# Starting every SBUF buffer of a hybrid FoX and mLSTM block at a multiple of 64 bytes, and loading its gate columns through two queues

## The chip, the core and the metric

The kernel runs on one core of one Trainium2 chip. The metric is the device time of one execution in microseconds (us), lower is better. A time is given as the median of several executions; the profile is one further execution, recorded by the hardware profiler.

## What is computed

One layer of a decoder block over 16 meta tokens and 512 real ones. Cut to what matters here:

```python
h = rms_norm(x, g_pre)                     # 528 x 1024
z = h @ w_in                               # 1024 x 14352, then split:
(fq, fk, fv, ff, fz, mqk, mv, mi, mf, mo, mz, ga, gb) = jnp.split(z, SPLIT_POINTS, axis=-1)
oa = forgetting_attention(fq, fk, fv, log_sigmoid(ff + b_fox_f))       # 8 heads of 128
ya = (oa * silu(fz)) @ w_a
mq, mk = jnp.split(silu(causal_conv(mqk, conv_w, conv_b)), 2, axis=-1)
hb = mlstm_scan(mq * 256 ** -0.5, mk, mv, mi + b_i, log_sigmoid(mf + b_f))   # 4 heads, values of 512
hb = rms_norm(sigmoid(mo) * hb, g_head)
yb = (hb * silu(mz)) @ w_b
return x + rms_norm((sigmoid(ga) * ya + sigmoid(gb) * yb) @ w_o, g_post)
```

The gates `ff`, `mi` and `mf` are 8, 4 and 4 columns of the input projection, 16 in all.

## The kernel before

**Precision.** Nearly every product is made of three matmuls (`mm3`, L128 to L131): each fp32 operand is split in a high part (a copy by ScalarE, names ending in `h`) and a low part (the rest, a subtraction by VectorE, names ending in `l`), and high x high, high x low and low x high are summed in PSUM. `wsplit` (L116) does this for a block of weights that `wload` (L102) fetched as `raw` tiles of 512 KB on SyncE's DMA queue. So a weight block is fetched, copied by ScalarE, subtracted by VectorE, and read by TensorE.

**Stages.** The start fetches the gain `g`, the token blocks `x` (into `yb`), the first value weights `wv_r` and the gate columns `wg_raw`; normalises block after block (`stat_part`, `scale_part`, `norm_part`: sum of squares on ScalarE, `rs` on GpSimd by a power, scaling on VectorE, transposes `tr` on TensorE, then `hh` and `hl`); and multiplies each block with the first 256 value columns and the 16 gate columns together (`pv`, 272 columns). The four mLSTM heads follow (convolved `pqk`, scores `ps`, values `pna`/`pnb`, gates `po` and `pz`, output `pyb`), then the FoX heads and the output projection `pout`.

**The meta tokens** have their own small operand `hm`, written by three engines (L513 to L515), and a projection `pvm` (`proj_m`, L168). `gn` collects the gate columns of the four real blocks and of the meta block; eight transposes (L542, L543) turn those of the real blocks into the rows `pgf` and `pgi`, two more (L545) those of the meta block into `pgm`, and one (L547) the convolution's taps into `gct`, copied to `gc`. From the rows VectorE and ScalarE work out the log gates (L555 to L566: `fx`, `gi`, exponential, logarithm), running sums (L571) and running maxima (L585), all of 12 partitions in `yb`. In the same stretch VectorE forms `l`, `t1l` and `t2l` (`st_tokens`, L181: sums of blocks of the tokens that later products use), and the low halves of the weights.

**Order.** A scheduler places the instructions of each engine after a cost model, except those wrapped in `pin`, which keep their program order. DMAs are issued in program order on the queue of the engine that starts them: SyncE for most, ScalarE for `g` and `wg_raw`.

**Buffers.** Tiles are laid out one behind another in SBUF. A statistics tile is one float per partition (4 bytes), a row of values is 514 floats. In the built kernel those lengths put the begin of the tiles behind them at other residues: `hh`, `hl`, `hm`, `big_h`, `big_l`, `qk1h`, `qk1l`, `vh` and the tail of `yb` views are at 32 beyond a multiple of 64 bytes, the weight tiles, `vl`, `y` and the `t1` to `t4` tiles at a multiple of 64. No DMA of this kernel is started by GpSimd.

Of the kernel before, what the change touches and what calls it, by code (L numbers as in the profile page):

```python
# [8 lines left out]
F32 = mybir.dt.float32  # L9
# [39 lines left out]
def tile_hybrid_block(ctx: ExitStack, tc: tile.TileContext, x, meta, norm_pre, norm_post, w_in, b_fox_f,  # L49
# [30 lines left out]
    gc = cp.tile([P, 96], F32, name="gc")  # L80
    col = cp.tile([P, NB + 2 * NCH, 12], F32, name="col")

# [235 lines left out]
    wg_raw = sb([P, KC, 16], F32, "t3l", "wg_raw", mw)  # L318
    for i in (1, 0):
        rows = slice(i * 512, i * 512 + 512)  # L320
        for o, c in ((0, C_FF), (8, C_MI)):
            nc.scalar.dma_start(wg_raw[:, 4 * i:4 * i + 4, o:o + 8], win[rows, c:c + 8].rearrange("(k p) n -> p k n", p=P))
# [15 lines left out]
    def stat_part(b):  # L338
        xt, n = xs[b]
        junk = sb([P, 2, 512], BF16, "vh", f"junk{b}")  # L340
        ss = sb([P, 1], F32, "ss", f"ss{b}", bufs=5)
        if b == 0:
            half = sb([P, 1], F32, "rs", "ss_half", bufs=5)
# [8 lines left out]
        rs = sb([P, 1], F32, "rs", f"rs{b}", bufs=5)  # L352
        pin(G.tensor_tensor(rs[:n], ss[:n], mhalf[:n], ALU.pow))
        rstd.append(rs)
# [34 lines left out]
    def v_tiles(h):  # L389
        vh = sb([P, NCH, MV + 2], F32R, "vh", f"vh{h}")  # L390
        vl = sb([P, NCH, MV + 2], F32R, "vl", f"vl{h}")
        vm = sb([P, MV + 2], F32R, "vm", f"vm{h}")
# [104 lines left out]

    b_fr = cp.tile([12, 1], F32, name="b_fr")
    b_ir = cp.tile([12, 1], F32, name="b_ir")
    V.memset(b_ir, 0.0)  # L500
# [27 lines left out]
    for b in range(NCH):  # L528
        pg = pv0[b]
        for d, o, n in ((0, 256, 8), (8, 268, 4), (20, 264, 4)):  # L530
            V.tensor_copy(gn[:, b, d:d + n], pg[:, o:o + n])
        S.activation(vh[:, b, 0:256], pg[:, 0:256], AF.Copy)
        V.tensor_tensor(vl[:, b, 0:256], pg[:, 0:256], f(vh[:, b, 0:256]), ALU.subtract)
    pm = psum1("pvm00")
    proj_m(pm[:, 0:NG], w0, NG)
# [3 lines left out]
    w_first.append(wsplit(lk, pin))  # L539
    pf, pi, pm2 = psum1("pgf"), psum1("pgi"), psum1("pgm")  # L540
# [39 lines left out]
    mp = cp.tile([12, NCH], F32, name="mp")  # L580
    V.tensor_tensor_scan(mx[:, 0:NM], a[:, 0:NM], a[:, 0:NM], 0.0, ALU.max, ALU.max)
# [128 lines left out]
    def mo_part(h):  # L710
        so = sb([P, NCH, MV], F32, "w", f"so{h}")
        pn = banks(f"po{h}", NCH)

        snaps = [so.rearrange("p s (m n) -> p m s n", m=2)[:, m] for m in range(2)]
        units = [(pn[m], pn[2 + m], snaps[m], slice(m * P, m * P + P)) for m in range(2)]
        st_products(st_wide(C_MO + h * MV, f"wo{h}"), units)

        dry = sb([P, 1], F32, "ss", f"dry{h}", bufs=5)
# [19 lines left out]
    def value_part(h, wpk, v, so, hts, chunks):  # L738
        wh, wl = wpk
        vh, vl, vm = v  # L740
        for c in chunks:
            pn = (psum1(f"pna{h}{c}"), psum1(f"pnb{h}{c}"))
            for u in (1, 0):
                o, n = u * 256, 256 + 2 * u
                for j in range(c + 1):
# [5 lines left out]
                         start=False, stop=True)  # L751
            r = sb([P, 1], F32, "r", f"r{h}{c}", bufs=4)
            V.tensor_scalar(r, pn[1][:, 256:257], -1.0, col[:, NB + NCH + c, 8 + h:9 + h], ALU.mult, ALU.max)
# [8 lines left out]
            junk = sb([P, MV], BF16, "y", f"mjunk{h}{c}", bufs=2)  # L762
            ss = sb([P, 1], F32, "ss", f"mss{h}{c}", bufs=5)
            S.activation(junk, ht, AF.Square, accum_out=ss)
            V.tensor_scalar(ss, ss, 1.0 / MV, EPS, ALU.mult, ALU.add)
            rs = sb([P, 1], F32, "rs", f"mrs{h}{c}", bufs=5)
            G.tensor_tensor(rs, ss, mhalf, ALU.pow)
# [39 lines left out]
    for h in range(MH):  # L807
        if pend is not None:
            bt = turn_part(*pend)
        q = conv_part(h, 0)  # L810
        k = conv_part(h, 1)
        if h:
# [3 lines left out]
        if h == 0:  # L816
            v = v0
            w1 = v_chunk(0, 1)
            ps = banks("pv01", 2)
# [81 lines left out]
    def prob_part(p, m, q, k):  # L901
# [7 lines left out]
        for c in range(NCH):  # L909
# [4 lines left out]
            parts = [(0, kn)] if kn <= 512 else [(0, HL), (HL, kn)]  # L914
            mn = sb([P, 2], F32, "mn", f"mn{h}{c}", bufs=4)
            for i, (s0, s1) in enumerate(parts):
# [194 lines left out]
```

## Time and profile before

| | |
|---|---|
| median of 3 executions | 963.04 us (962.84 to 963.21) |
| the profiled execution | 963.74 us |
| its span in the trace | 962.0 us |
| TensorE busy | 944.3 us, 98% of the span, 5720 matmuls |
| VectorE busy | 572.3 us, 59% |
| ScalarE busy | 439.5 us, 46% |
| GpSimd busy | 140.1 us, 15% |
| bytes read from HBM | 86.95 MB, 93 GB/s over the span |

Engines are named PE (TensorE's matmuls), PEld (its weight loads), DVE (VectorE), ACT (ScalarE), POOL (GpSimd); SPq and ACTq are the queues of SyncE and ScalarE that start DMAs. In a timeline row the first number is the start and the second the duration, both in us; brackets at the end tell how long the engine had been idle and what released it. The duration of a matmul is its way through the array; the rate of a series is read from start to start.

### The profile page before, as it was taken

How to read it: one execution, taken by the hardware profiler on the slowest of the kernel's cores; microseconds unless marked ns; L12 is line 12 of the kernel's file. 1: busy time of each engine (PE TensorE's matmuls, PEld its weight loads, DVE VectorE, ACT ScalarE, POOL GpSimd, SP SyncE). 2: the span in 40 equal slices, each digit the busy share in tenths (PEclk: the TensorE clock that was granted, in tenths of full speed). 3: DMA queues.
4: the chain of work that ended last, by engine and by line, in shares of the span. 5: the costliest groups of instructions: out<-in, count | busy, mean ns of one | idle time of the engine just before them, and what ended most of it. 6: DMA issues, size and time to landing. Idle time of an engine off the chain costs nothing.

```text
span 962.0 us, 14294 instructions
## 1 busy us (share of the span) xinstructions
PE 944.3 (98%) x5720; PEld 837.4 (87%) x5720; DVE 572.3 (59%) x966; ACT 439.5 (46%) x740; POOL 140.1 (15%) x186
## 2 busy tenths in 40 slices
PE   8999899999999999999999999999999999999997
PEld 6998899889998899988999888898888888888887
DVE  6898588447786288862788445445345454444433
ACT  5646456436564255562555224456235365422331
POOL 3054100122001220011112010123111012100000
PEclk9999899999999999999999999999999999999999
DMA  7222143303323123322224242333332332523202
GB/s 224 91 70 77 45 132 100 88 22 96 118 73 105 60 66 111 110 59 84 81 79 166 87 137 66 106 89 111 88 96 94 88 87 68 175 88 103 95 22 89
DMA packets 71469, 90.05 MB, mean 94 GB/s; under 512 B 4965, under 2 KB 56261, under 8 KB 71402
## 3 DMA queue, kind: packets, MB, share of 16 engines
q1 hardware_dynamic: 69288, 89.06, 30.2%
q8 instruction: 45, 0.74, 0.3%
q10 hardware_dynamic: 2114, 0.07, 0.1%
q14 instruction: 22, 0.18, 0.1%
HBM read 86.95 MB, written 2.16 MB: 93 GB/s over the span
## 4 chain that ended last, share of the span: by engine, by line
PE 89%; DVE 4%; ACT 2%; issue 1%; POOL 1%; DMA 1%; ACTq 0%; POOLq 0%; DVEq 0%; SPq 0%
PE pyb L131 3%; PE pyb L129 3%; PE pyb L130 3%; PE pz L130 3%; PE pz L131 3%; PE pz L129 3%; PE pv L129 3%; PE pv L131 3%; PE pv L130 3%; PE pqk L129 2%; PE pqk L131 2%; PE pqk L130 2%; PE po L130 2%; PE po L129 2%; PE po L131 2%; PE pfk L131 2%
## 5 line engine op out<-in xcount | busy, mean ns | idle before, releaser
L928 POOL TENSOR_SCALAR pn<-lt,rsum 128x128 f32<-128x128 f32 x32 | 23.1, 723 | 213.2 <-DVE rsum L926 213.2
L129 PE MATMUL pyb<-bh,wb_h 128*128 128x512 f32 x128 | 50.8, 397 | 0.0
L131 PE MATMUL pyb<-bh,wb_l 128*128 128x512 f32 x128 | 50.7, 396 | 0.0
L130 PE MATMUL pyb<-bl,wb_h 128*128 128x512 f32 x128 | 50.7, 396 | 0.0
L130 PE MATMUL pv<-wv_l,hh 128*128 128x512 f32 (+1 forms) x128 | 47.2, 368 | 1.7 <-DVE wv_l L123 1.5
L129 PE MATMUL pv<-wv_h,hh 128*128 128x512 f32 (+1 forms) x128 | 46.9, 367 | 0.0
L131 PE MATMUL pv<-wv_h,hl 128*128 128x512 f32 (+1 forms) x128 | 46.7, 365 | 0.0
L660 DVE SCALAR_TENSOR_TENSOR y<-z,gc,y 128x512 f32<-128x512 f32 (+1 forms) x48 | 35.9, 752 | 2.2 <-ACT y L653 1.5
L129 PE MATMUL pqk<-hh,wk_h 128*128 128x264 f32 x128 | 36.4, 285 | 0.0
L129 PE MATMUL pfk<-hh,wfk_h 128*128 128x264 f32 x128 | 36.4, 284 | 0.0
L131 PE MATMUL pfk<-hh,wfk_l 128*128 128x264 f32 x128 | 36.4, 284 | 0.0
L129 PE MATMUL pqk<-hh,wq_h 128*128 128x258 f32 x128 | 36.4, 284 | 0.0
L131 PE MATMUL pqk<-hh,wk_l 128*128 128x264 f32 x128 | 36.3, 284 | 0.0
L130 PE MATMUL pqk<-hl,wk_h 128*128 128x264 f32 x128 | 36.3, 284 | 0.0
L130 PE MATMUL pfk<-hl,wfk_h 128*128 128x264 f32 x128 | 36.3, 283 | 0.0
L130 PE MATMUL pqk<-hl,wq_h 128*128 128x258 f32 x128 | 36.0, 282 | 0.0
L131 PE MATMUL pqk<-hh,wq_l 128*128 128x258 f32 x128 | 36.0, 282 | 0.0
L129 PE MATMUL pout<-wo_h,mh 128*128 128x256 f32 (+1 forms) x96 | 30.6, 319 | 0.0
L131 PE MATMUL pout<-wo_h,ml 128*128 128x256 f32 (+1 forms) x96 | 30.5, 318 | 0.0
L130 PE MATMUL pout<-wo_l,mh 128*128 128x256 f32 (+1 forms) x96 | 30.4, 317 | 0.0
L925 ACT ACTIVATE lt<-lt,mn 128x144 f32<-128x144 f32 (+3 forms) x32 | 18.4, 574 | 24.7 <-DVE mn L920 24.6
L130 PEld LDWEIGHTS pv<-wv_l,hh 128*128 128x128 f32 x128 | 24.1, 188 | 6.3 <-DVE wv_l L123 2.1
(979 smaller groups left out, 3299.8 us busy)
## 6 DMA issues: line engine op xcount, KB each, us to landing
wv_r<-in_w_in_dram SPq DMA_DIRECT2D x16, 512.0 KB, 4.5
wo_r<-in_w_in_dram SPq DMA_DIRECT2D x16, 512.0 KB, 4.5
wz_r<-in_w_in_dram SPq DMA_DIRECT2D x16, 512.0 KB, 3.8
wb_r<-in_w_b_dram SPq DMA_DIRECT2D x16, 512.0 KB, 3.5
ab<-d_na SPq DMA_DIRECT2D x8, 672.0 KB, 4.0
wq_r<-in_w_in_dram SPq DMA_DIRECT2D x8, 512.0 KB, 3.8
wk_r<-in_w_in_dram SPq DMA_DIRECT2D x8, 512.0 KB, 3.7
wfq_r<-in_w_in_dram SPq DMA_DIRECT2D x8, 512.0 KB, 3.9
```

The lines of the kernel that those rows point to most:

```text
L129: T.matmul(ps, ah, bh, start=start, stop=False, **kw)
L130: T.matmul(ps, ah, bl, start=False, stop=False, **kw)
L131: T.matmul(ps, al, bh, start=False, stop=stop, **kw)
L660: V.scalar_tensor_tensor(y[:, t0:L], z[:, m, t0 + j:L + j], gc[:, j * 16 + mi:j * 16 + mi + 1], y[:, t0:L], ALU.mult, ALU.add)
L925: S.activation(lt[:, 0:kn], lt[:, 0:kn], AF.Exp, bias=mn[:, li:li + 1], scale=-1.0, accum_out=rsum)
L928: G.tensor_scalar(pn[:, o:o + P].rearrange("p (g t) -> p g t", g=4), lt[:, 0:32].unsqueeze(1).to_broadcast([P, 4, 32]), rsum, None, ALU.mult)
```

## The change

- A helper `line` gives every small tile a length of 16 floats (64 bytes) or a multiple, and the rows of the value tiles `vh`, `vl`, `vm` get 16 more floats where they had 2. GpSimd's DMA scratch area is 1 KB instead of 16 KB. In the built kernel every buffer then begins at a multiple of 64 bytes.
- The four DMAs that fetch `wg_raw` are split: the two of the rows 512 to 1023 stay on ScalarE's queue, the two of the rows 0 to 511 are started by SyncE, behind `x` block 1.
- The six gate transposes of the first three blocks stand ahead of the meta projection `pvm`, those of the fourth behind it, as all eight did.
- The second block of value weights of head 0 (`v_chunk(0, 1)`) is split ahead of the key convolution instead of behind it.

```diff
+    def line(pool, name, n=1, parts=P, **kw):
+        return pool.tile([parts, -(-n // 16) * 16], F32, name=name, **kw)[:, 0:n]
...
-    col = cp.tile([P, NB + 2 * NCH, 12], F32, name="col")
+    col = line(cp, "col", (NB + 2 * NCH) * 12).rearrange("p (b r) -> p b r", r=12)
...
-    for i in (1, 0):
+    def gate_load(q, i):
         rows = slice(i * 512, i * 512 + 512)
         for o, c in ((0, C_FF), (8, C_MI)):
-            nc.scalar.dma_start(wg_raw[:, 4 * i:4 * i + 4, o:o + 8], ...)
+            q.dma_start(wg_raw[:, 4 * i:4 * i + 4, o:o + 8], ...)
+    gate_load(nc.scalar, 1)
...
             load0 = wload(win, 0, KC, C_MV, 256, "wv00")
+        elif b == 1:
+            gate_load(nc.sync, 0)
...
-        ss = sb([P, 1], F32, "ss", f"ss{b}", bufs=5)
+        ss = line(wk, f"ss{b}", 1, tag="ss", bufs=5)
...
-        vh = sb([P, NCH, MV + 2], F32R, "vh", f"vh{h}")
+        vh = sb([P, NCH, MV + 16], F32R, "vh", f"vh{h}")[:, :, 0:MV + 2]
...
+    gate_rows(range(3))
     pm = psum1("pvm00")
     proj_m(pm[:, 0:NG], w0, NG)
...
-    for b in range(NCH):
-        T.transpose(pf[0:12, b * P:b * P + P], gn[:, b, 0:12], ident)
-        T.transpose(pi[0:12, b * P:b * P + P], gn[:, b, 12:24], ident)
+    gate_rows(range(3, NCH))
...
         q = conv_part(h, 0)
+        if h == 0:
+            w1 = v_chunk(0, 1)
         k = conv_part(h, 1)
...
-            w1 = v_chunk(0, 1)
...
-    nc = _bacc.Bacc("TRN2", target_bir_lowering=False, num_devices=1)
+    nc = _bacc.Bacc("TRN2", target_bir_lowering=False, num_devices=1, dynamic_dma_scratch_size=1024)
```

The lists of instructions differ only in the first part of the kernel. Lines of the changed kernel have numbers that are 4 to 15 higher.

SyncE's queue at the start, before (`yb` are the blocks of `x`):

```order
L326 DMA yb<-in_x_dram 128x1024
L108 DMA wv_r_106<-in_w_in_dram 128x4x256
L108 DMA wv_r_108<-in_w_in_dram 128x4x256
L326 DMA yb<-in_x_dram 128x1024 x3
L331 DMA xm<-in_meta_tokens_dram 16x1024
```

and in the changed kernel:

```order
L333 DMA yb<-in_x_dram 128x1024
L112 DMA wv_r_104<-in_w_in_dram 128x4x256
L112 DMA wv_r_106<-in_w_in_dram 128x4x256
L333 DMA yb<-in_x_dram 128x1024
L327 DMA wg_raw<-in_w_in_dram 128x4x8 x2
L333 DMA yb<-in_x_dram 128x1024 x2
L340 DMA xm<-in_meta_tokens_dram 16x1024
```

Two small DMAs have come between `x` block 1 and block 2. ScalarE's first instructions are otherwise the same, with two of them gone ahead of its table load.

VectorE behind the meta projection (`gn<-pvm` are the meta gates, `wk_l` the low half of the key weights), before:

```order
L537 COPY gn<-pvm_424 128x4 x2
L201 TENSOR_TENSOR l_525<-l_525,hl 128x1024
L533 TENSOR_TENSOR vl_398<-pv_3_122,vh_397 128x256
L178 TENSOR_TENSOR vm_399<-pvm_424,vm_399 32x256
L123 TENSOR_TENSOR wk_l_448<-wk_r_169,wk_h_446 128x1024
L123 TENSOR_TENSOR wk_l_452<-wk_r_171,wk_h_450 128x1024
L548 COPY gc<-gct 128x96
L554 COPY yb<-pgm 12x256
L557 TENSOR_SCALAR yb<-pgi,b_ir 12x512
```

and in the changed kernel:

```order
L554 COPY gn<-pvm_433 128x4 x2
L571 TENSOR_SCALAR yb<-pgi,b_ir 12x512
L542 TENSOR_TENSOR vl_398<-pv_3_122,vh_397 128x256
L182 TENSOR_TENSOR vm_399<-pvm_433,vm_399 32x256
L562 COPY gc<-gct 128x96
L568 COPY yb<-pgm 12x256
L127 TENSOR_TENSOR wk_l_457<-wk_r_169,wk_h_455 128x1024
L127 TENSOR_TENSOR wk_l_461<-wk_r_171,wk_h_459 128x1024
```

The three copies of gate rows have moved ahead of the key weights, and L201 behind them. VectorE where the logarithm of the gates comes back from ScalarE (L564 reads it), before:

```order
L202 TENSOR_TENSOR l_525<-l_525,hl 128x1024
L209 SCALAR_TENSOR_TENSOR l_526<-l_525,hh 128x1024
L561 TENSOR_SCALAR yb<-yb 12x528
L210 TENSOR_TENSOR l_526<-l_526,hl 128x1024
L564 SCALAR_TENSOR_TENSOR yb<-yb 12x528
```

and in the changed kernel (L578 reads it):

```order
L205 TENSOR_TENSOR l_525<-l_525,hl 128x1024
L206 TENSOR_TENSOR l_525<-l_525,hl 128x1024
L575 TENSOR_SCALAR yb<-yb 12x528
L213 SCALAR_TENSOR_TENSOR l_526<-l_525,hh 128x1024
L200 TENSOR_TENSOR t1l<-l_525,t1h 128x1024
L578 SCALAR_TENSOR_TENSOR yb<-yb 12x528
```

Behind the request for the logarithm (L561, L575) one long instruction stood before, and two stand now. From some twenty instructions further on, VectorE's list is the same again, the two `wv_l` of the second value block among it.

## Rows read from the trace of the kernel before

**Rows 1.** The page: busy time of each engine, and the chain by engine.
```profile
PE 944.3 (98%) x5720; PEld 837.4 (87%) x5720; DVE 572.3 (59%) x966; ACT 439.5 (46%) x740; POOL 140.1 (15%) x186
...
PE 89%; DVE 4%; ACT 2%; issue 1%; POOL 1%; DMA 1%; ACTq 0%; POOLq 0%; DVEq 0%; SPq 0%
```

**Rows 2.** Waits of PE: what for, us in total, times, longest.
```profile
PE pnb L747 <- ACT wh L694: 1.7, 2, 1.2
PE pv L130 <- DVE wv_l L123: 1.5, 1, 1.5
...
PE pnb L749 <- DVE wl L696: 0.8, 1, 0.8
```

**Rows 3.** Timeline of all engines, the first 8 us.
```profile
1.28 2.49 ACTq L322 DMA_DIRECT2D wg_raw<-in_w_in_dram  x4
...
2.83 3.78 PE L317 MATMUL pg<-g,ones 1*128 1x512 f32 x4
3.80 1.28 ACT L345 ACT_TABLE_LOAD   x1 [3.80 <-issue]
...
4.27 0.69 DVE L346 CUSTOM_DVE_ANT_0 junk_half<-yb 128x512 bf16<-128x512 f32 x1 [2.70 <-DMA yb<-in_x_dram]
...
5.09 0.63 ACT L345 ACTIVATE junk<-yb 128x512 bf16<-128x512 f32 x1
...
6.93 1.41 DVE L361 SCALAR_TENSOR_TENSOR yb<-yb,rs,pg 128x512 f32<-128x512 f32 x2 [0.74 <-POOL rs L353]
...
7.74 1.97 PE L368 MATMUL tr<-ident,yb 128*128 128x128 f32 x8 [1.13 <-DVE yb L361]
```

**Rows 4.** The gate columns: issue to landing of their four DMAs.
```profile
DMA to landing us min/median/max: 8.2/8.7/9.1
```

**Rows 5.** The gate columns' DMA queue, first 30 us: packets, MB, share of 16 engines.
```profile
q10 hardware_dynamic: 2114, 0.07, 4.4%
```

**Rows 6.** Timeline of PE: the meta projection, and the first gate transposes behind it.
```profile
30.60 0.36 PE L172 MATMUL pvm<-w0h_big_h,hm 128*128 128x272 f32 x1 [0.86 <-POOL hm L515]
...
32.69 0.27 PE L542 MATMUL pgf<-ident,gn 128*12 128x128 f32 x1
32.79 0.27 PE L543 MATMUL pgi<-ident,gn 128*12 128x128 f32 x1
```

**Rows 7.** Timeline of DVE between 35 and 61 us.
```profile
35.57 2.36 DVE L123 TENSOR_TENSOR wk_l<-wk_r,wk_h 128x1024 fp32r<-128x1024 f32 x2 [0.47 <-ACT wk_h L121]
...
42.14 1.21 DVE L210 TENSOR_TENSOR l<-l,hl 128x1024 f32<-128x1024 f32 x1
44.26 0.70 DVE L564 SCALAR_TENSOR_TENSOR yb<-yb 12x528 f32<-12x528 f32 x1 [0.91 <-ACT yb L562]
...
59.41 1.19 DVE L123 TENSOR_TENSOR wv_l<-wv_r,wv_h 128x1024 fp32r<-128x1024 f32 x1
```

**Rows 8.** By stretch: us, busy time (instructions) of PE, PEld, DVE, ACT, POOL; PEclk, DMA share, GB/s.
```profile
36.00:62.00 26.00, 24.33 (x200) 23.92 (x199) 25.02 (x50) 16.11 (x27) 10.56 (x8) 1.00 0.14 44
62.00:100.00 38.00, 38.00 (x228) 33.23 (x227) 33.56 (x37) 22.27 (x40) 15.25 (x12) 1.00 0.35 106
...
104.00:112.00 8.00, 6.79 (x31) 6.40 (x32) 5.55 (x15) 1.85 (x5) 0.10 (x1) 0.57 0.00 1
```

**Rows 9.** Timeline of PE: begin of a `pz` series, and of the next two.
```profile
120.67 0.28 PE L129 MATMUL pz<-t2h,wz00d_h 128*128 128x256 f32 x1
...
122.08 0.28 PE L129 MATMUL pz<-hh,wz00d_h 128*128 128x256 f32 x1
...
123.50 0.28 PE L747 MATMUL pnb<-vh,wh 128*128 128x258 f32 x1
```

**Rows 10.** Timeline of PE: the output projection, 256 columns.
```profile
934.38 0.28 PE L129 MATMUL pout<-wo_h,mh 128*128 128x256 f32 x1
...
935.28 0.28 PE L131 MATMUL pout<-wo_h,ml 128*128 128x256 f32 x1
...
936.84 0.28 PE L129 MATMUL pout<-wo_h,mh 128*128 128x256 f32 x1
```

More of the change, by code (lines that the diff above doesn't have):

```diff
@@ L318, in tile_hybrid_block @@
     wg_raw = sb([P, KC, 16], F32, "t3l", "wg_raw", mw)
-    for i in (1, 0):
+    def gate_load(q, i):
         rows = slice(i * 512, i * 512 + 512)
         for o, c in ((0, C_FF), (8, C_MI)):
-            nc.scalar.dma_start(wg_raw[:, 4 * i:4 * i + 4, o:o + 8], win[rows, c:c + 8].rearrange("(k p) n -> p k n", p=P))
+            q.dma_start(wg_raw[:, 4 * i:4 * i + 4, o:o + 8], win[rows, c:c + 8].rearrange("(k p) n -> p k n", p=P))
+    gate_load(nc.scalar, 1)
     xs = []
@@ L340, in stat_part @@
         junk = sb([P, 2, 512], BF16, "vh", f"junk{b}")
-        ss = sb([P, 1], F32, "ss", f"ss{b}", bufs=5)
+        ss = line(wk, f"ss{b}", 1, tag="ss", bufs=5)
         if b == 0:
-            half = sb([P, 1], F32, "rs", "ss_half", bufs=5)
+            half = line(wk, "ss_half", 1, tag="rs", bufs=5)
             junk2 = sb([P, 512], BF16, "y", "junk_half", bufs=2)
@@ L351, in stat_part @@
         pin(V.tensor_scalar(ss[:n], ss[:n], 1.0 / DM, EPS, ALU.mult, ALU.add))
-        rs = sb([P, 1], F32, "rs", f"rs{b}", bufs=5)
+        rs = line(wk, f"rs{b}", 1, tag="rs", bufs=5)
         pin(G.tensor_tensor(rs[:n], ss[:n], mhalf[:n], ALU.pow))
@@ L389, in v_tiles @@
     def v_tiles(h):
-        vh = sb([P, NCH, MV + 2], F32R, "vh", f"vh{h}")
-        vl = sb([P, NCH, MV + 2], F32R, "vl", f"vl{h}")
-        vm = sb([P, MV + 2], F32R, "vm", f"vm{h}")
+        vh = sb([P, NCH, MV + 16], F32R, "vh", f"vh{h}")[:, :, 0:MV + 2]
+        vl = sb([P, NCH, MV + 16], F32R, "vl", f"vl{h}")[:, :, 0:MV + 2]
+        vm = sb([P, MV + 16], F32R, "vm", f"vm{h}")[:, 0:MV + 2]
         G.memset(f(vh[:, :, MV:MV + 2]), 1.0)
@@ L495, in tile_hybrid_block @@
     w_first = [wsplit(lq, pin)]
-    b_fr = cp.tile([12, 1], F32, name="b_fr")
-    b_ir = cp.tile([12, 1], F32, name="b_ir")
+    b_fr = line(cp, "b_fr", parts=12)
+    b_ir = line(cp, "b_ir", parts=12)
     V.memset(b_ir, 0.0)
@@ L533, in tile_hybrid_block, with gate_rows @@
         V.tensor_tensor(vl[:, b, 0:256], pg[:, 0:256], f(vh[:, b, 0:256]), ALU.subtract)
+    pf, pi, pm2 = psum1("pgf"), psum1("pgi"), psum1("pgm")
+    def gate_rows(bs):
+        for b in bs:
+            T.transpose(pf[0:12, b * P:b * P + P], gn[:, b, 0:12], ident)
+            T.transpose(pi[0:12, b * P:b * P + P], gn[:, b, 12:24], ident)
+    gate_rows(range(3))
     pm = psum1("pvm00")
@@ L579, in tile_hybrid_block @@
         V.tensor_copy(ac[:, c, k0:k1], a[:, k0:k1])
-    mp = cp.tile([12, NCH], F32, name="mp")
+    mp = line(cp, "mp", NCH, 12)
     V.tensor_tensor_scan(mx[:, 0:NM], a[:, 0:NM], a[:, 0:NM], 0.0, ALU.max, ALU.max)
@@ L716, in mo_part @@
         st_products(st_wide(C_MO + h * MV, f"wo{h}"), units)
-        dry = sb([P, 1], F32, "ss", f"dry{h}", bufs=5)
+        dry = line(wk, f"dry{h}", 1, tag="ss", bufs=5)
         pin(S.activation(dry, mhalf, AF.Sigmoid))
@@ L751, in value_part @@
                          start=False, stop=True)
-            r = sb([P, 1], F32, "r", f"r{h}{c}", bufs=4)
+            r = line(wk, f"r{h}{c}", 1, tag="r", bufs=4)
             V.tensor_scalar(r, pn[1][:, 256:257], -1.0, col[:, NB + NCH + c, 8 + h:9 + h], ALU.mult, ALU.max)
@@ L762, in value_part @@
             junk = sb([P, MV], BF16, "y", f"mjunk{h}{c}", bufs=2)
-            ss = sb([P, 1], F32, "ss", f"mss{h}{c}", bufs=5)
+            ss = line(wk, f"mss{h}{c}", 1, tag="ss", bufs=5)
             S.activation(junk, ht, AF.Square, accum_out=ss)
             V.tensor_scalar(ss, ss, 1.0 / MV, EPS, ALU.mult, ALU.add)
-            rs = sb([P, 1], F32, "rs", f"mrs{h}{c}", bufs=5)
+            rs = line(wk, f"mrs{h}{c}", 1, tag="rs", bufs=5)
             G.tensor_tensor(rs, ss, mhalf, ALU.pow)
@@ L914, in prob_part @@
             parts = [(0, kn)] if kn <= 512 else [(0, HL), (HL, kn)]
-            mn = sb([P, 2], F32, "mn", f"mn{h}{c}", bufs=4)
+            mn = line(wk, f"mn{h}{c}", 2, tag="mn", bufs=4)
             for i, (s0, s1) in enumerate(parts):
@@ L923, in prob_part @@
             li = len(parts) - 1
-            rsum = sb([P, 1], F32, "r", f"rsum{h}{c}", bufs=4)
+            rsum = line(wk, f"rsum{h}{c}", 1, tag="r", bufs=4)
             S.activation(lt[:, 0:kn], lt[:, 0:kn], AF.Exp, bias=mn[:, li:li + 1], scale=-1.0, accum_out=rsum)
@@ L1049, in tile_hybrid_block @@
     og = yb.rearrange("p (b u) t -> p b (u t)", b=NCH)
-    oss = cp.tile([P, NCH, 3], F32, name="oss")
-    opre = cp.tile([P, NCH], F32, name="opre")
+    oss = line(cp, "oss", NCH * 3).rearrange("p (b i) -> p b i", i=3)
+    opre = line(cp, "opre", NCH)
     def out_end(ps, b, c0, n, i):
@@ L1075, in tile_hybrid_block @@
             if u == 3:
-                rs = sb([P, 1], F32, "rs", f"ors{b}", bufs=5)
+                rs = line(wk, f"ors{b}", 1, tag="rs", bufs=5)
                 V.scalar_tensor_tensor(rs, oss[:, b, 2:3], 1.0 / DM, opre[:, b:b + 1], ALU.mult, ALU.add)
```

3 lines of the change are left out of this document (1 added, 2 removed).

## The prediction

> **What bounds the kernel now.** First the page: PE is busy 944.3 of 962.0 us and the chain that ended last runs through it for 89% [rows 1]. So most of the time is the rate at which PE issues matmuls, and what is left for an edit of the order is the 18 us in which it does not. Next the list of PE's waits, to see which of them the edits touch: the longest single ones are 1.5 us on a `wv_l`, 1.2 us on a `wh` and 0.8 us on a `wl` [rows 2]; the start has one of 1.13 us and the meta projection one of 0.86 us [rows 3, 6]. Then the stretches by window: between 36 and 62 us it is VectorE that is full, 25.02 of 26 us, while PE waits; from 62 to 100 PE is busy throughout; from 104 to 112 the granted clock is 0.57 on average, a stretch at the lower level behind PE's waits for `wh` and `wl` [rows 8, 2]. So in the first 100 us the end is set by a chain through DVE, ACT and POOL, and behind it by PE's rate.
>
> **The start.** ScalarE's queue issues four gate DMAs from 1.28 for 2.49 us, and only then its table load begins, 3.80 to 5.08; the first sum of squares follows at 5.09 [rows 3]. VectorE's half of the same sum begins at 4.27, when `x` block 0 has landed. With two issues less, about half of 2.49, the table load runs from about 2.5 to 3.8, ahead of the landing, and ScalarE's half begins with VectorE's: 5.09 - 4.27 = 0.82 us earlier. The scaling at 6.93 and the transposes at 7.74 hang on it and shift by 0.82. What would be late next is the gain in PSUM: PE's `pg` matmuls end at 2.83 + 3.78 = 6.61; the second half of the scaling, 6.93 + 0.70 - 0.82 = 6.81, still comes behind them, with 0.20 to spare. I count **-0.8**.
>
> The two DMAs come to SyncE between `x` blocks 1 and 2, so all that is queued there stands behind them: `x` 2 and 3, `xm` and the key and query weights. Their issue costs SyncE half of 2.49 us, but the three blocks behind them took 4.89 us to issue, waiting for earlier transfers, so it lies beside that wait. Their packets cost little: the queue that carried them had 2114 packets in 4.4% of 30 us of 16 engines [rows 5], which is 1.3 us on each engine, half of it, 0.66 us, now ahead of block 2. Bounds: 0 and +0.66; I take 0, since block 1 sits ahead of them and the clock of the stretch behind is PE's own. The gates themselves took 8.2 to 9.1 us from issue to landing [rows 4] and are read behind 12 us.
>
> Here a rule of the Trainium skill speaks against the edit: "DMA: Bandwidth & Descriptors", section "Issuing engines are not separate DMA queues", says that DMAs started by different engines run on the same 16 DMA engines, and that spreading them saves only the sequencer's time for issuing. By it nothing lands sooner, and the whole gain is the ScalarE time above; the trace of before cannot show more.
>
> **Gate transposes.** Six of them move into the 0.86 us in which PE waits for `hm`; they follow each other by 0.10 us [rows 6], so 0.6 us less work stands behind `pvm`. PE's gain from this is not the kernel's: before 60.65 PE waits 1.5 us for `wv_l` [rows 2], so whatever PE gains earlier turns into waiting there, unless VectorE comes sooner too.
>
> **VectorE to 60 us.** VectorE ends its second `wv_l` at 59.41 + 1.19 = 60.60 and PE goes on at once [rows 7, 2]. Its list up to there holds the same instructions in another order, so its end moves by the shift of its begin (-0.8) and by the idle time that the order takes out. There are two idle stretches: 0.47 before `wk_l`, waiting for ScalarE, and 0.91 before L564, waiting for the logarithm behind a table load [rows 7]. In the new order three short copies (0.3 to 0.7 us each) stand ahead of `wk_l`, with one long sum gone behind it; and behind the request for the logarithm stand two long instructions, 2.4 us, where one of 1.21 stood. The second idle stretch is then covered but for about 0.1; the first I take as unchanged to slightly smaller, since ScalarE's `wk_h` waits for the PE that ends 0.4 to 0.6 sooner. From 1.38 us of idle time some 0.5 are left: **-0.8** more, bounds 0 (new waits of the same size) and -1.4 (all gone). Where does it go? Through `wv_l` to PE at 60.65, and through VectorE's next instructions to the scores at 100: PE has no slack from 62 to 100 and the waits at 100 to 106 are of the same chain, so both shift alike. What is late next are the same two waits, 1.2 for `wh` and 0.8 for `wl`, at an earlier time. Moving `v_chunk(0, 1)` brings ScalarE's copies of `wv` ahead of `t2h`; `wv_l` keeps its place in VectorE's list, so I count 0.
>
> **Alignment on DVE, ACT and POOL.** An instruction on buffers that begin 32 beyond a multiple of 64 takes as long as one on buffers that do not: 1.21 us with `hl`, 1.19 with weights only, both 128x1024 [rows 7]. 0, and the same for ScalarE's and GpSimd's. A scratch area that nothing uses costs nothing.
>
> **Alignment on PE.** This touches 900 us of the span, so a small share counts. I went by starts. Twelve matmuls on `t2`, which begins at a multiple of 64, take 122.08 - 120.67 = 1.41 us, the twelve on `hh`, at 32, 123.50 - 122.08 = 1.42 [rows 9]: 117.5 and 118.3 ns each, 0.8 ns apart. I take the same for wider ones. Some 2000 of the 5720 matmuls stream from a buffer that moves from 32 to 0 (1386 of 512 columns); the stationary side moves in another 2035, where I see none. 2000 x 0.7 = **-1.4** us; bounds 0 (0.8 ns is near the resolution) and, from one place, more: in `pout` eight matmuls from 934.38 take 0.90 us, 112 ns each, and the thirteen behind take 1.56, 120 ns [rows 10]. The eight read `mh` tiles at a multiple of 64, the others partly not. If all 1000 matmuls of 256 to 272 columns that change gained the 7 ns, it would be -7. Against that stand the `pz` rows, aligned on both sides at 117.5.
>
> The Trainium skill, "SBUF — State Buffer", the box on cachelines under "Door 1: The DMA port swizzle", gives SBUF lines of 16 bytes; every buffer here began at a multiple of 16 already, so by it the padding would give 0, the sum -1.6, and the second rival below. The rows differ by 0.8 ns, little enough that I keep that case.
>
> **The sum.** -0.8 - 0.8 - 1.4 = -3.0 us. The profiled execution took 963.74, its span of 962.0 and 1.7 around it; the change would bring it to 960.7. The median lies 0.7 under the profiled one: 963.04 - 3.0 = **960.0 us**.
>
> **The rivals.**
>
> *A shorter stretch at the lower clock.* PE ran at the lower of its two levels (1.2 instead of 2.4 GHz) for nearly 7 us behind the waits at 100 to 106; it is busy 6.79 of the 8 us there [rows 8], so half of some 6 us, 3 us, is what the clock costs. If the waits get shorter than 1.2 and 0.8, the clock may not fall, or for less long; a wait that takes its place (ScalarE's `wh`, VectorE's `wl` are then later than PE) gives about 1 back. Against it: waits that shift with their chain keep their length. Time: 960.0 - 2 = 958.0. Chance 0.15.
>
> *The padding does nothing.* For it: the 16-byte reading, and 0.8 ns at the edge of what starts resolve. Then only order and start are left, 963.04 - 1.6 = 961.4, and 962.2 if VectorE's order gives nothing either. This is no change that can be told. Chance 0.23.
>
> *The padding does much.* If `pout`'s 7 ns are the rule, -7 in place of -1.4: 954.5. Against it the `pz` rows. Chance 0.07.
>
> *Slower: a second stretch at the lower clock.* PE gains 0.8 at the start and 0.6 at the transposes, so it reaches its wait for `wv_l` sooner. If VectorE's new order gains nothing, say because the gate rows now wait for PE's last transposes with `wk_l` and all else queued behind, that wait grows from 1.5 to 1.5 + 1.4 = 2.9 us, more than the waits of 1.2 and 0.8 together behind which the clock fell at 104. A like stretch at 60 costs 3 us, nothing of the start is kept, and if the padding does nothing either: 963.04 + 3 = 966.0. It decides from where VectorE gains under some 0.6 us. Against it: the list of VectorE has the same instructions and fewer stalls, and 1.5 us at 60 did not lower the clock. Chance 0.10.
>
> **How the numbers follow.** Forecast 0.45, the four rivals 0.15, 0.23, 0.07 and 0.10. A measurement of this kernel can tell about 0.2%, 1.9 us, so faster means under 961.1, slower over 965.0. Faster: 0.45 + 0.15 + 0.07, less 0.02 for the forecast's upper edge, 0.65; the padding that does nothing falls in the middle, 0.25; slower 0.10. The forecast's own range by its bounds is 958.9 (idle time all gone, 0.5 of padding more) to 961.0. To hold 8 in 10 it takes in the shorter stretch below, 957.8, and the case of no padding above, 962.2; left out are 0.07 below and 0.10 above.
>
> **What would show it.** ScalarE's table load ends before 4 us and the first transposes begin at 6.9: the start. VectorE's second `wv_l` ends near 59.0 and the wait before L564's counterpart is under 0.3: the order. Starts in `pz` on `hh` 117.5 ns apart, as on `t2`: the padding; the stretch from 120 to 950 us, 830 us with hardly a wait, must be 1.2 us shorter. I am wrong if `x` 2 lands later than 12 us and ScalarE waits for it; if the clock column shows a stretch at the lower level at 60, or none at 104; or if the long stretch is shorter by several us, which would say that 64 bytes matter to PE far more than the `pz` rows do.

## The result, and the profile of the changed kernel

The changed kernel takes 958.20 us, median of 4 executions (957.83 to 959.97), against 963.12 us for the kernel before in the same comparison (962.84 to 964.25). The ratio is 0.995, 95% interval 0.9933 to 0.9968: 4.9 us less, 0.5%. The prediction was 960.0, in a range of 957.8 to 962.2. The sign and the place of the start held; the padding was worth twice what the prediction gave it, VectorE's order a little less, and 0.6 us came from a place that the prediction did not look at. That the 958.20 lies inside the range is partly luck, as the section on the prediction says.

The profiled execution, 959.97 us with a span of 958.1, was the longest of the four, for a reason that the list of PE's waits shows. The columns are what is waited for, the total in us, the times, the longest:

```profile
PE ps L133 <- ACT yb L721: 2.1, 1, 2.1
PE pv L134 <- DVE wv_l L127: 1.5, 1, 1.5
...
PE pnb L761 <- ACT wh L708: 0.7, 1, 0.7
PE pnb L763 <- DVE wl L710: 0.6, 1, 0.6
```

The first row is a wait at the scores that was 0.5 us before. The chain leads from there to a transfer of `wz_r` issued at 65.31 that took 7.4 us to land, where the chain of before had one of 5.3. So the same kernel was profiled again (the last experiment, called *again*: 958.19 us median, span 956.8). Its page begins like this:

```profile
span 956.8 us, 14295 instructions
...
PE 941.1 (98%) x5720; PEld 835.7 (87%) x5720; DVE 572.4 (60%) x966; ACT 439.5 (46%) x740; POOL 140.6 (15%) x186
```

The busy times of DVE, ACT and POOL are those of [rows 1] to 0.5 us; PE has 3.2 us less, for the same 5720 matmuls. PE's waits in that profile:

```profile
PE pnb L761 <- ACT wh L708: 1.7, 2, 1.2
PE pv L134 <- DVE wv_l L127: 1.5, 1, 1.5
...
PE pnb L763 <- DVE wl L710: 0.8, 1, 0.8
PE ps L133 <- ACT yb L721: 0.4, 1, 0.4
PE tr L377 <- DVE yb L370: 0.4, 1, 0.4
```

The long ones are those of [rows 2], of the same length: they have moved with the chain, not gone. The 2.1 us belonged to one execution. All comparisons of traces below use the second profile where the first is disturbed.

The start, as in [rows 3] (start, duration, engine, line):

```profile
1.28 0.96 ACTq L327 DMA_DIRECT2D wg_raw<-in_w_in_dram  x2
...
2.27 1.28 ACT L354 ACT_TABLE_LOAD   x1 [2.27 <-issue]
...
4.27 0.63 ACT L354 ACTIVATE junk<-yb 128x512 bf16<-128x512 f32 x1 [0.72 <-DMA yb<-in_x_dram]
...
6.17 1.41 DVE L370 SCALAR_TENSOR_TENSOR yb<-yb,rs,pg 128x512 f32<-128x512 f32 x2 [0.74 <-POOL rs L362]
...
6.97 1.33 PE L377 MATMUL tr<-ident,yb 128*128 128x128 f32 x5 [0.36 <-DVE yb L370]
```

The table load ends at 3.55 and ScalarE waits for `x` block 0, which lands at 4.27 as before. The scaling begins at 6.17 instead of 6.93 and the transposes at 6.97 instead of 7.74.

VectorE and PE at 60 us, as in [rows 6, 7]:

```profile
42.77 0.70 DVE L578 SCALAR_TENSOR_TENSOR yb<-yb 12x528 f32<-12x528 f32 x1 [0.48 <-ACT yb L576]
...
58.01 1.19 DVE L127 TENSOR_TENSOR wv_l<-wv_r,wv_h 128x1024 fp32r<-128x1024 f32 x1
```

```profile
59.25 0.38 PE L134 MATMUL pv<-wv_l,hh 128*128 128x256 f32 x1 [1.47 <-DVE wv_l L127]
```

The second `wv_l` begins at 58.01 instead of 59.41, so 1.40 us sooner, and PE goes on at 59.25 instead of 60.65. PE's wait for it has kept its length. VectorE waits 0.48 us for the logarithm where it waited 0.91, and the 0.47 before `wk_l` is gone.

From a matmul of the first `pz` to the last one of the kernel PE has hardly a wait. Before:

```profile
117.83 0.28 PE L129 MATMUL pz<-hh,wz00c_h 128*128 128x256 f32 x1
...
954.88 0.28 PE L131 MATMUL pout<-wo_h,ml 128*128 128x256 f32 x1
```

and in the second profile of the changed kernel:

```profile
116.42 0.28 PE L133 MATMUL pz<-hh,wz00c_h 128*128 128x256 f32 x1
...
950.38 0.28 PE L135 MATMUL pout<-wo_h,ml 128*128 128x256 f32 x1
```

837.05 us before, 833.96 after: 3.09 us less for the same matmuls. The first profile of the changed kernel gives 833.90. This stretch is the measure for the padding in what follows, called *the long stretch*. The granted clock is 1.00 throughout it, in all profiles, and PE's few waits in it (for `fvm` 1.3 us, for `fsz` 1.1 us) are the same before and after.

And the end. VectorE's last instruction before:

```profile
956.92 1.41 DVE L1081 SCALAR_TENSOR_TENSOR yb<-yb,ors,xr 128x512 f32<-128x512 f32 x2 [0.66 <-POOL ors L1078]
```

and after:

```profile
952.41 1.41 DVE L1096 SCALAR_TENSOR_TENSOR yb<-yb,ors,xr 128x512 f32<-128x512 f32 x2 [0.66 <-POOL ors L1093]
```

It ends at 958.33 and 953.82, and the spans, to two digits, at 961.96 and 956.82: 3.63 us of issue, landing and closing before, 3.00 after, 0.63 less.

### The profile page after: what moved, and what is told of

Same layout as the page of the kernel before. It is cut to its first block, busy times and chain, and to the rows that moved or that the text cites. A ratio compares the mean times of both kernels' runs of the same rounds, so it can differ in the third digit from the quotient of the medians.

```text
span 958.1 us, 14295 instructions
## 1 busy us (share of the span) xinstructions
PE 942.0 (98%) x5720; PEld 835.7 (87%) x5720; DVE 572.5 (60%) x966; ACT 439.7 (46%) x740; POOL 140.4 (15%) x186
## 4 chain that ended last, share of the span: by engine, by line
PE 90%; DVE 4%; ACT 2%; DMA 1%; issue 1%; POOL 1%; POOLq 0%; DVEq 0%; ACTq 0%; SPq 0%
PE pyb L133 3%; PE pyb L135 3%; PE pyb L134 3%; PE pz L134 3%; PE pz L133 3%; PE pz L135 3%; PE pqk L135 3%; PE pqk L133 3%; PE pv L133 3%; PE pv L135 3%; PE pqk L134 3%; PE pv L134 3%; PE po L134 2%; PE po L135 2%; PE po L133 2%; PE pfk L135 2%
```

## The experiments

Theories. **A**: the padding shortens the distances between PE's matmuls, 3.1 us, whatever comes before. **B**: the padding does nothing, the gain belongs to the order. **C**, formed after the first four runs: the distances follow from how the operands' addresses lie to each other, and multiples of 64 bytes have nothing to do with it; **D** is its strict form (only distances between buffers count), **E** a rival to it (the half of a 128-byte line counts too). The kernel before ran beside each; its medians were 963.5 to 963.7. A single execution carries about 1 us of the clock (last section), so the traces decide on parts below that.

**Padding alone.** The kernel before with the helper and the small scratch area; its instruction lists are those of before.

```diff
+    def line(pool, name, n=1, parts=P, **kw):
+        return pool.tile([parts, -(-n // 16) * 16], F32, name=name, **kw)[:, 0:n]
...
-        ss = sb([P, 1], F32, "ss", f"ss{b}", bufs=5)
+        ss = line(wk, f"ss{b}", 1, tag="ss", bufs=5)
...
+        vh = sb([P, NCH, MV + 16], F32R, "vh", f"vh{h}")[:, :, 0:MV + 2]
```

> The kernel before with the padding and the small scratch area alone: every buffer at a multiple of 64 bytes, the lists of all engines as before. Theory A (the padding lets PE issue its matmuls at shorter distances, 3.1 us over the 830 us from 120 to 950, whatever comes before): the first 100 us as before, the long stretch 3 us shorter, 960.0 us. Theory B (the padding does nothing, the shorter distances belong to the new order, by another phase between PE and the transfers that run beside it): 963.0 us. The prediction's own term for the padding was 1.4 us: 961.6.

960.49 us, ratio 0.9973 (0.9962 to 0.9983). PE is where it was before until 100 us (0.1 us apart at 60 us), and the long stretch, taken from the same two matmuls in each kernel, takes 833.86 us, 3.19 less. A, not B.

**Order and queue alone.** The changed kernel without padding.

```diff
-        ss = line(wk, f"ss{b}", 1, tag="ss", bufs=5)
+        ss = sb([P, 1], F32, "ss", f"ss{b}", bufs=5)
...
-    nc = _bacc.Bacc("TRN2", target_bir_lowering=False, num_devices=1, dynamic_dma_scratch_size=1024)
+    nc = _bacc.Bacc("TRN2", target_bir_lowering=False, num_devices=1)
```

> The changed kernel without padding and with the scratch area of before: the gate columns in two queues, the six transposes and the value chunk moved, buffers at 32 beyond 64 as before. Theory A: only the start and VectorE's order count, 1.1 us at 60 us as in the changed kernel's trace, PE's distances as before: 962.0 us. Theory B: the whole gain is here, 958.2 us.

961.63 us, ratio 0.9984 (0.9975 to 0.9993). The long stretch is 837.05, as before to the last digit. PE is 0.24 us sooner at 30 us and 0.82 sooner at 60, so the order from 30 to 60 us gives 0.58. In that execution `x` block 0 landed at 4.62 instead of 4.27 and `g` half a microsecond later, which took part of the start. The span is 1.6 us shorter where PE's last matmul is only 1.0 sooner: the rest is the end of the kernel.

**All buffers 32 bytes further.**

```diff
+    shift = cp.tile([P, 8], F32, name="shift")
+    G.memset(shift, 0.0)
     ident = cp.tile([P, P], F32, name="ident")
```

> The changed kernel with a tile of 32 bytes ahead of all others: padding, pitches and order as in it, but every buffer begins 32 beyond a multiple of 64. Theory A in the form that the begin decides: PE's distances as before the change or longer (the weights are off too), 961.3 us or more. Theory A in the form that only the difference between the two operands of a matmul decides, or that the pitch of padded rows or the lower addresses do it: 958.2 us. Theory B: 958.2 us.

958.5 us, ratio 0.9951 (0.9939 to 0.9964), and the long stretch 833.82 us. Every buffer is 32 beyond a multiple of 64, the residue that the padding was to remove, and the kernel is as fast as the changed one. The begin at a multiple of 64 is not what gives the time. A falls in the form that the prediction used.

**The gate queue alone.**

```diff
+    gate_load(nc.scalar, 1)
...
+        elif b == 1:
+            gate_load(nc.sync, 0)
```

> The kernel before with only the two gate DMAs moved to SyncE's queue. Theory A, that the start shifts by 0.5 us as in the changed kernel's trace and carries to the end: transposes at 7.2 us instead of 7.74, 962.5 us. Rival: the wait for wv_l at 60 us takes it up and nothing is left, 963.0 us, or PE's wait for the scores at 100 us grows because the weights' transfers land no sooner, 963.0 us or more.

962.61 us, ratio 0.9993 (0.9984 to 1.0001), 1.1 us by the medians, within the interval no safe difference. The trace: ScalarE's half of the sum begins at 4.40, PE is 0.50 us sooner from 14 us on and still 0.50 sooner at 60 and at the last matmul. PE's wait for `wv_l` did not take it up, since VectorE came sooner by the same. The span is 1.1 us shorter; 0.6 of that lies behind the last matmul.

**The small scratch area alone.**

```diff
-    nc = _bacc.Bacc("TRN2", target_bir_lowering=False, num_devices=1)
+    nc = _bacc.Bacc("TRN2", target_bir_lowering=False, num_devices=1, dynamic_dma_scratch_size=1024)
```

> The kernel before with the small scratch area alone: every buffer 15,360 bytes lower, their residues and distances unchanged. Theory C (PE's distances between matmuls follow from how the addresses of the operands lie to each other, and nothing else): no change, 963.1 us, the stretch from 120 to 948 as before to 0.1 us. Rival (the lower addresses or the freed area do it): 960 us.

963.53 us, ratio 0.9998 (0.9989 to 1.0007), long stretch 837.06. Nothing, as C had it. Its part in the change is room: the longer value rows need it.

**hh and hl 32 bytes off, the rest at multiples of 64.**

```diff
+    s1 = cp.tile([P, 8], F32, name="s1")
+    G.memset(s1, 0.0)
     hh = cp.tile([P, KC, L], F32R, name="hh")
     hl = cp.tile([P, KC, L], F32R, name="hl")
+    s2 = cp.tile([P, 8], F32, name="s2")
+    G.memset(s2, 0.0)
```

> The changed kernel with a tile of 32 bytes ahead of hh and another behind hl: hh and hl begin 32 beyond a multiple of 64, all else at multiples of 64, with distances among the rest as in the changed kernel. Theory C in the form that 32 against 64 between the two operands is what costs: the series that use hh (pv, pfz, pgb, pfq, pfv, part of po, pz) go back to the distances of before, about 1.2 of the 3.1 us are lost, 959.4 us; po on t keeps 113 ns. Rival (64 has nothing to do with it): the series on hh change either way, by 1 us or less, 957.5 to 959.

960.03 us, ratio 0.9964 (0.995 to 0.9978). From the `pz` to the last matmul:

```profile
115.91 0.28 PE L137 MATMUL pz<-hh,wz00c_h 128*128 128x256 f32 x1
...
951.83 0.28 PE L139 MATMUL pout<-wo_h,ml 128*128 128x256 f32 x1
```

835.92 us, 2.0 of the 3.1 us lost. Summed by product, the series that read `hh` (`pv`, `pfz`, `pgb`, `pfq`, `pfv`, `pga`) lost 1.2 us, as C's form had it. Against it, `po` lost 1.3 us more and `pyb` became 0.4 us shorter than in the changed kernel: `po` on `t` lost its short distances as well, though neither operand of it moved against the other. The rows are shown below, behind the last shift.

**The t and wz tiles 64 bytes further.** Every buffer stays at a multiple of 64.

```diff
     mw = c1.enter_context(tc.tile_pool(name="mlstm", bufs=1))
+    s1 = mw.tile([P, 16], F32, name="s1")
+    G.memset(s1, 0.0)
```

> The changed kernel with a tile of 64 bytes ahead of the t and wz tiles: every buffer still begins at a multiple of 64, but those lie 64 further from all others. Theory that the multiple of 64 decides: no change, 958.2 us. Theory C, that the distance decides: po on t leaves 113 ns for about 118, 1.1 us lost, and the series on wz and hh change too, 959.3 us or another number in 957 to 961.

959.68 us, ratio 0.9959 (0.9944 to 0.9974).

```profile
115.75 0.28 PE L135 MATMUL pz<-hh,wz00c_h 128*128 128x256 f32 x1
...
951.59 0.28 PE L137 MATMUL pout<-wo_h,ml 128*128 128x256 f32 x1
```

835.84 us: 1.9 of the 3.1 us lost with every buffer at a multiple of 64, 1.65 of it in `po` and 0.27 in `pz`, the two products that read the moved tiles. So the multiple is neither needed (all at 32) nor enough.

**The value rows alone**, with the scratch area that they need.

```diff
-        vh = sb([P, NCH, MV + 2], F32R, "vh", f"vh{h}")
+        vh = sb([P, NCH, MV + 16], F32R, "vh", f"vh{h}")[:, :, 0:MV + 2]
```

> The kernel before with the longer value rows and the small scratch area, the small tiles as before. hh, hl and the weights keep the distances of before, so do hh and the FoX tiles; what lies behind vh moves. Theory C: hh against weights (pv, pfz, pgb, pfq, pfv, pga) as before, pna, pnb and po on t may change; 961.5 to 963. Rival (the pitch of the value rows is the cause): pna and pnb shorter, and nothing else, below 0.3 us. Rival (the small tiles): 963.1 us, all as before.

964.54 us, ratio 1.001 (1.0001 to 1.002): by 0.1% slower, just outside its interval, and longer than any of the three expectations.

```profile
117.60 0.28 PE L129 MATMUL pz<-hh,wz00c_h 128*128 128x256 f32 x1
...
955.61 0.28 PE L131 MATMUL pout<-wo_h,ml 128*128 128x256 f32 x1
```

838.01 us, 0.96 longer than before. `po` is 0.69 us longer and `pz` 0.61, whose `t` tiles lie behind the value rows; `pyb` is 0.72 shorter; `pna` and `pnb`, which read the rows themselves, are 0.04 shorter each. The pitch of the rows is not the gain.

**The small tiles alone**, with the scratch area.

```diff
-        ss = sb([P, 1], F32, "ss", f"ss{b}", bufs=5)
+        ss = line(wk, f"ss{b}", 1, tag="ss", bufs=5)
```

> The kernel before with the small tiles padded and the small scratch area, the value rows as before: hh, hl, the weights and all up to vl begin at multiples of 64 as in the changed kernel, what lies behind the value rows at 32 beyond. With the value rows alone the long stretch was 1.0 us longer, with both 3.2 us shorter. If the small tiles do the work: the series of hh against weights as in the changed kernel, 1.2 us, and po on t, pyb and pout undecided: 961.5 to 963 us. If only both together do it: 963 us or more.

962.73 us, ratio 0.9993 (0.9983 to 1.0002). The long stretch takes 836.82 us, 0.23 less. Series by series, from the starts: `pv`, `pfz`, `pgb` and `pfq` on `hh` are as short as in the changed kernel (1.0 us together), and `po` and `pout` are longer than before by 0.84. Neither half gives the 3.1 us and the two together do, so the gain is no sum of the two halves; that each half moves tiles that the other leaves in place fits this.

**All buffers 64 bytes further.**

```diff
+    shift = cp.tile([P, 16], F32, name="shift")
+    G.memset(shift, 0.0)
     ident = cp.tile([P, P], F32, name="ident")
```

> The changed kernel with a tile of 64 bytes ahead of all others: every buffer still begins at a multiple of 64, and all distances between buffers are as in the changed kernel. Theory D (only the distances between operands decide, as the kernel shifted by 32 bytes suggests): no change, 958.2 us, po on t at 113 ns. Theory E (the half of a 128-byte line in which an operand begins counts as well, as the kernel with hh at 32 suggests, in which po on t lost its 113 ns although its distance was kept): po on t back to 118, 1.1 us lost, pyb 0.4 us shorter as there; 959 us.

958.21 us, ratio 0.9944 (0.993 to 0.9959).

```profile
116.14 0.28 PE L135 MATMUL pz<-hh,wz00c_h 128*128 128x256 f32 x1
...
950.09 0.28 PE L137 MATMUL pout<-wo_h,ml 128*128 128x256 f32 x1
```

833.95 us: no change, as D had it, and E falls. A shift of everything by 32, 64 or 15,360 bytes costs nothing; a shift of some buffers against others by 32 or 64 costs 2 us. Product by product the same holds: in the five kernels without padding each product takes the same time in the long stretch to 0.01 us, and in padding alone, the changed kernel (both profiles) and the two shifts of everything to 0.06 us.

The clearest series shows it: 48 matmuls of `po` on `t3` and `t1`, from the first to the start of the series behind it. Before, and in the changed kernel:

```profile
217.47 0.28 PE L129 MATMUL po<-wo1b_h,t3h 128*128 128x256 f32 x1
...
223.13 0.28 PE L129 MATMUL po<-wo1d_h,hh 128*128 128x256 f32 x1
```

```profile
215.80 0.28 PE L133 MATMUL po<-wo1b_h,t3h 128*128 128x256 f32 x1
...
221.24 0.28 PE L133 MATMUL po<-wo1d_h,hh 128*128 128x256 f32 x1
```

5.66 and 5.44 us, 117.9 and 113.3 ns each; both operands began at multiples of 64 in both kernels. All 64 bytes further, then `t` and `wz` alone 64 further, then `hh` 32 further:

```profile
215.52 0.28 PE L135 MATMUL po<-wo1b_h,t3h 128*128 128x256 f32 x1
...
220.96 0.28 PE L135 MATMUL po<-wo1d_h,hh 128*128 128x256 f32 x1
```

```profile
215.18 0.29 PE L135 MATMUL po<-wo1b_h,t3h 128*128 128x256 f32 x1
...
220.89 0.28 PE L135 MATMUL po<-wo1d_h,hh 128*128 128x256 f32 x1
```

```profile
215.33 0.28 PE L137 MATMUL po<-wo1b_h,t3h 128*128 128x256 f32 x1
...
220.99 0.28 PE L137 MATMUL po<-wo1d_h,hh 128*128 128x256 f32 x1
```

5.44, 5.71 and 5.66 us. In the third the two operands kept their distance, and beside `hh` and `hl` only `ident` and a constant, which lie ahead of `hh`, moved against them. So the series on `t` depends on where a buffer lies that it does not read; `hh` is an operand of the matmuls just ahead.

Two simple readings of that fail in the traces. One is that other engines, busy beside PE, set the pace. The second half of the same product, `po` on `t4` and `t2`, ran beside quite other work. The two stretches of 48 matmuls in the second profile of the changed kernel, busy time (instructions) of PE, PEld, DVE, ACT and POOL, then PEclk, DMA share and GB/s:

```profile
215.80:221.24 5.44, 5.44 (x50) 5.44 (x49) 4.62 (x5) 3.33 (x4) 0.00 (x0) 1.00 0.09 15
224.09:229.53 5.44, 5.44 (x51) 5.44 (x49) 3.21 (x3) 3.41 (x5) 2.33 (x3) 1.00 0.52 162
```

With a DMA share of 0.52 instead of 0.09, and POOL at work, the second takes the same 5.44 us, and so do the like stretches of the next two heads. The other reading is that a series takes over the pace of the one ahead. The 24 matmuls on `hh` ahead of `t3`, and those ahead of `t4`, end where the next row begins:

```profile
212.98 0.28 PE L133 MATMUL po<-wo1a_h,hh 128*128 128x256 f32 x1
...
224.09 0.28 PE L133 MATMUL po<-wo1e_h,t4h 128*128 128x256 f32 x1
```

From 212.98 to 215.80 they take 117.5 ns each and from 221.24 to 224.09 118.6 (2.846 us by the starts to the nanosecond), and behind both the series on `t` takes 113.3. How the address of a buffer acts on a series that does not read it, and which distance is good, was not found.

**Transposes and value chunk alone.**

```diff
+    gate_rows(range(3))
     pm = psum1("pvm00")
...
         q = conv_part(h, 0)
+        if h == 0:
+            w1 = v_chunk(0, 1)
         k = conv_part(h, 1)
```

> The kernel before with the six gate transposes ahead of the meta projection and the value chunk ahead of the key convolution, nothing else. By the difference between the two kernels with the gate queue (0.5 us) and with queue and order (0.82 to 1.1 us): VectorE's second wv_l and PE behind it 0.4 us sooner at 60 us, 962.7 us. The prediction had 0.8 us here. Rival (the order gives nothing by itself): 963.1 us.

962.8 us, ratio 0.9994 (0.9984 to 1.0004), so by the clock no safe difference. The trace: in that execution PE is 0.20 us late at the start, 0.02 sooner at 42 us and 0.40 sooner at 60 and at the last matmul 0.55, so the order gives 0.60 by 60 us. The long stretch is 837.05.

**The changed kernel once more**, without an edit.

> The changed kernel once more, for a second profile. In its first one a transfer of wz at 65 us took 7.4 us and held PE back by 2.1 us at the scores. If that belongs to the kernel it comes again, with a span of 958 us; if it was that execution, the transfer takes 5.1 to 5.3 us as in the other kernels, PE reaches 118 us about 2.2 us sooner than before the change, and the span is 956 us.

958.19 us, ratio 0.9946 (0.9931 to 0.9961), span 956.8. The slow transfer of `wz_r` did not come again; PE reaches the first `pz` 1.4 us sooner than before, not 2.2. The wait at the scores fell from 2.1 to 0.4 us, but the waits behind it, for `wh` and `wl`, grew from 1.3 to 2.5 in total, back to what they were before the change. The length at the lower clock does not differ: both profiles have 6.8 us of it.

## Why the prediction was right, and where it was not

The 958.20 us lie inside the stated range, and that is partly luck. The forecast's own range by its bounds was 958.9 to 961.0, and the measured time is outside it. The stated range reached down to 957.8 for the rival of a shorter stretch at the lower clock, and it was the padding that filled that room, at more than twice its term, and the end of the kernel, which had no term.

Term by term, in us, from the traces:

| term | predicted | measured | from |
|---|---|---|---|
| start | -0.8 | -0.77, -0.52, -0.50 | second profile, first profile, gate queue alone |
| VectorE to 60 us | -0.8 | -0.63, -0.58, -0.60 | second profile, order, transposes alone |
| padding on PE | -1.4 | -3.09, -3.15, -3.19 | second profile, first profile, padding alone |
| end of the kernel | 0 | -0.63 | second profile |
| sum | -3.0 | -5.1; -4.9 | second profile; the medians |

*The start* went in the way that was worked out. ScalarE's half of the sum begins with the landing of block 0; where that landed later (4.52 in the first profile, 4.40 with the queue alone) the gain is 0.5. The start varies by itself: the first transposes begin at 7.70 to 7.94 in the six profiles with four gate DMAs on ScalarE's queue, and at 6.97 to 7.32 in the eight with two. On average PE is 0.6 us sooner at 14 us, so the 0.77 of the second profile is the best case. `x` 2 and 3 behind the gate DMAs were not late: no engine waits for them in the changed kernel. The rule of the Trainium skill, "DMA: Bandwidth & Descriptors", "Issuing engines are not separate DMA queues", that only issue time is saved, fits the gain at the start. By it nothing lands sooner, and there the trace differs: the gate columns landed 7.0 us after their issue where it was 8.7 [rows 4]. Nobody waited for them.

*The gate transposes*: the wait of 0.86 before `pvm` is 0.21 in the changed kernel, and PE's gain from it did go into waiting at `wv_l`, which kept 1.47 of 1.54 us because VectorE came sooner by as much. The step held.

*VectorE's order*: of the two idle stretches the prediction left 0.5 us, and the trace has 0.48, though in another place: the wait for the logarithm kept 0.48 where 0.1 was expected, and the one before `wk_l` went. The gain is 0.6, not 0.9 as that would give: VectorE has a new wait of 0.13 us for the gate rows at 32.49, and its instructions between the first scaling and `wv_l` take 0.15 us more (47.19 us busy instead of 47.04).

*The padding* is the step that failed, in size and in kind. The prediction put it at 2000 matmuls by 0.7 ns, from `pz` on `t2` and on `hh` [rows 9], and gave the stationary side nothing. In the changed kernel the 504 matmuls of `po` alone gave 1.18 us, since 288 of them, on `t`, went from 117.8 to 113.3 ns (1.3 us; those on `hh` lost 0.1), with the same residue mod 64 on both sides before and after; `pz` on `t` stayed at 117.5 to 118. The other products gave 0.4 us or less each, and one, `pfo`, lost 0.2. So what [rows 9] showed as a matter of 32 against 64 was one of many distances. The very series that gave the price went the other way, here in the second profile:

```profile
119.26 0.28 PE L133 MATMUL pz<-t2h,wz00d_h 128*128 128x256 f32 x1
...
120.67 0.28 PE L133 MATMUL pz<-hh,wz00d_h 128*128 128x256 f32 x1
...
122.10 0.28 PE L761 MATMUL pnb<-vh,wh 128*128 128x258 f32 x1
```

The twelve on `t2` take 1.41 us as before and the twelve on `hh`, now at a multiple of 64, 1.43: 119 ns, where the prediction's sign for the padding was 117.5. [Rows 10] had the right warning, 112 ns beside 120 within one product, and the prediction used it only as a bound; the reason it gave, `mh` tiles at a multiple of 64, does not hold either, since with all buffers there the same eight matmuls take 118 ns each (929.97 to 930.91 in the second profile). Its last sign of being wrong, a long stretch shorter by several us, came true, but not for the reason that it names, 64 bytes: all buffers at 32 give the same.

By the sentence of the Trainium skill on lines of 16 bytes ("SBUF — State Buffer", under "Door 1: The DMA port swizzle") the padding gives 0. The long stretch, 3.1 us shorter, speaks against reading it as a rule for PE's pace here; the shift of all buffers by 32 bytes, which leaves the long stretch as it was, agrees with it as far as the begin alone goes.

*The rivals.* The padding that does nothing: excluded by padding alone. The padding that does much, 7 us by the `pout` pace: not so, though the pace exists. The second stretch at the lower clock at 60 us: not there; the wait for `wv_l` did not grow. The shorter stretch at the lower clock behind 102 us came in some kernels' profiles. The windows, with PEclk as the third number from the end: the changed kernel (second profile), the padding alone, the small tiles alone:

```profile
102.00:110.00 8.00, 6.63 (x29) 6.04 (x30) 5.77 (x15) 1.66 (x4) 0.10 (x1) 0.58 0.00 1
```

```profile
102.00:113.00 11.00, 8.17 (x50) 7.47 (x50) 7.71 (x20) 3.63 (x8) 0.67 (x2) 0.84 0.07 24
```

```profile
102.00:113.00 11.00, 7.72 (x56) 6.90 (x57) 8.52 (x22) 3.34 (x8) 0.66 (x2) 1.00 0.04 12
```

6.8 us at the lower level in the first as in [rows 8], 3.4 us in the second, none in the third, behind the same waits of 1.2 and 0.8 us. All five profiles without any padding show the full length; of the nine with all or part of it one shows the full length, one two of 3.4 us, six one of 3.4 us and one none. The single executions say more. In the profiles a mean granted clock of 0.996 or more goes with less than the full length. The kernel before has such a clock in 37 of 63 executions, and the kernels with all or part of the padding in 47 of 54. So the stretch varies without any change, and may be shorter more often with the padding. The executions of the kernel before at 0.996 or more are 0.8 us shorter by their medians than the others; with these shares that makes an estimated 0.2 us. Whether the padding does it stays open. The long stretch does not contain it.

*The end* was not in the prediction. From the start of the last matmul to the end of the span it takes 7.07 to 7.10 us in the six profiles of kernels with four gate DMAs on ScalarE's queue, and 6.41 to 6.45 in the eight with two on SyncE's. The queue alone shows it, so it belongs to that edit. The last output goes out on SyncE's queue 0.10 us behind VectorE's end before and 0.03 after, and the span ends 3.53 us and 2.97 us behind that issue. The two landings that the traces have among the last outputs change places: the third from last in 2.02 us before and 2.36 after, the second from last in 2.39 and 2.04, and likewise in every other profile of the two groups. The landing of the last itself is not in the traces, and why two more DMAs at the start of a queue change any of this is not known.

## What to carry to other kernels

On a kernel in which one engine is busy for 98% of the span, compare the starts of two of its instructions, one behind the last early wait and the last one, between two builds before anything else: here that one difference, 837.05 against 833.96 us, was the same to 0.15 us in every build with the same distances between buffers, while single executions of one kernel differed by 1 us and more. A new layout of buffers changed that stretch by -0.4 to +0.1 per cent here, so a change of a tile's size should be timed as a change of layout, not put down to its alignment. A DMA taken from the front of a compute engine's queue is worth its issue time only up to the next thing that engine waits for: here 1.5 us of issue went, and 0.5 to 0.8 were gained.

## What the runs showed of the hardware

PE's pace in a series depends on how its buffers, and at least one that it does not read, lie to each other: `po` on `t` took 113.3, 117.8, 119 or 120 ns for 256 columns with the same list of instructions, the same in all three heads, whatever the other engines did. Shifts of all buffers by 32, 64 and 15,360 bytes left the long stretch the same to 0.15 us (833.82 and 833.95 beside 833.90 and 833.96, 837.06 beside 837.05). One transfer of 512 KB took 7.4 us where the same one took 5.0 to 5.5 in the other thirteen profiles, and PE waited 2.1 us behind it; by the spans, 958.1 beside 956.8, that execution hid 1.3 us of the gain. The mean granted clock of the kernel before varied from 0.993 to 0.998 over its executions, with times from 966.0 to 962.4.
